# Attention scores of one head: the four products of 128 rows first, then the four of 64 rows

## The chip, the cores and the metric

The kernel runs on one NeuronCore of a Trainium2 chip. The metric is the device time of one execution in microseconds (us), as the median of several executions. Five engines work side by side, each through its own queue in order: TensorE (PE in the profile, with its weight loads as PEld), VectorE (DVE), ScalarE (ACT), GpSimd (POOL) and SyncE (SP), which here issues the DMA transfers. Products of TensorE land in PSUM, from where DVE and ACT read them.

## The reference

One layer of a decoder on 512 prompt positions and 8 single sample positions (520 columns in all), D_MODEL 1024: half a SwiGLU feed-forward block, a mixer, and half a SwiGLU block again. The mixer projects to a gated convolution (512 channels) and to attention with 8 heads of 64 channels. Three dilated patterns over the same keys are combined by their softmax masses, so for the prompt the kernel computes one masked softmax per head, in which a bias carries the logarithm of how many patterns see a key:

```
res = [dilated_band_prompt(q, k, v, w, d) for (w, d) in PATTERNS]
attn = combine_patterns([r[0] for r in res], [r[1] for r in res])
...
x = x + jnp.concatenate([y_c, y_a], axis=-1) @ w_out
```

Everything is float32, and the results have to be close to float32 accuracy.

## The kernel before, in words

Activations lie channels first: a tile has 128 channels on the partitions and positions in the columns. float32 products are made of three faster ones: each operand is split into a high part and a remainder (`hi` by ACT at L108, `lo` by DVE at L109), and `mm3` (L121 to L123) adds high·high, high·low and low·high in PSUM. Weights come through `load_w`, four raw buffers deep.

The mixer's order is written out in `ORDER`: `q`, `k`, `v`, `t` prepare a pair of heads, `C` are the three steps of a convolution block, `S` and `V` the sample's scores and values, `M` its softmax, `R` the norm of the convolution group, `O` the output projection of that group, and `A` and `B` the first and the second head of a pair. The heads come as A0, B0, A1, B1, A2, B2, A3, B3. A step with `!` is issued on TensorE only behind what was traced before it. For the rest, a scheduler that simulates a timeline sets the order on each engine, with earlier steps ahead of later ones when both are ready; the order it finds is then fixed. At the end stand `R B3 O0 O1 V1 O2 V2 V3 O3 ... O7`, then `rstd_rows` for the norm of the attention group (its chain ends in `r2`, L187) and `out_proj(4, r2)`, whose results wait for `r2` at L747.

One head (`head`) goes like this. The scores of query block `ib` (128 positions) against the keys up to its end (256, 256, 384 and 512 columns) are two products into one PSUM tile: L567 takes 128 rows, the high part of the head's 64 query channels twice over against the keys' high part and remainder; L568 takes 64 rows, the queries' remainder against the keys' high part. Blocks 0 and 1 share the tile `s01`, blocks 2 and 3 have `s2` and `s3`. The softmax of a block is a DVE pass at L575 (scale, mask, row minimum), an exponential at L577, a reciprocal and a multiplication. The transposes of L586 go to `pt` tiles, from there ACT and DVE make a high part and a remainder (L589, L590), and L594 to L597 multiply with the values into the tile `o`, which L598 and L599 read out.

All of `s01`, `s2`, `s3`, the three `pt` tiles and `o` share one tag of three PSUM buffers:

```
psS = s2.enter_context(tc.tile_pool(name="psS", bufs=3, space=PSUM, reuse_waits="tile"))
```

The tile of `R` (`one_s`, named `nps`) and that of `M` (`tp`) use the same three buffers. `R` sums a norm at L193, spreads its result back at L160, and ACT reads the tile out at L199, twice.

Of the kernel before, what the change touches and what calls it, by code (L numbers as in the profile page):

```python
# [13 lines left out]
P = 128  # L14
# [37 lines left out]
def tile_step(ctx: ExitStack, tc: tile.TileContext, xT, w0, w1a, w3a, w2a, w_in, w_out, w1b, w3b, w2b,  # L52
# [3 lines left out]
    V, A, G, PE, SP = nc.vector, nc.scalar, nc.gpsimd, nc.tensor, nc.sync  # L56
# [400 lines left out]
    with ExitStack() as st:  # L457
# [9 lines left out]
        with ExitStack() as s2:  # L467
# [90 lines left out]
            def head(e, q2, ql, k2, v2, at):  # L558
                rows = ROWS[e]
                s01 = psS.tile([P, 512], F32, name="s01", tag="s")  # L560
                s2_ = psS.tile([P, 512], F32, name="s2", tag="s")
                s3_ = psS.tile([P, 512], F32, name="s3", tag="s")
                dst = [s01[:, 0:256], s01[:, 256:512], s2_[:, 0:384], s3_[:, 0:512]]
                for ib in range(4):
                    n = max(256, P * (ib + 1))
                    i = slice(ib * P, (ib + 1) * P)
                    PE.matmul(dst[ib], lhsT=q2[e][:, i], rhs=k2[e][:, :n], start=True, stop=False)  # L567
                    PE.matmul(dst[ib], lhsT=ql[rows, i], rhs=k2[e][rows, :n], start=False, stop=True)  # L568
                mx = sm.tile([P, 4], F32, name="mx", tag="mx")
                z = sm.tile([P, 4], F32, name="z", tag="z")  # L570
                pr = []
                for ib in range(4):
                    n = P * (ib + 1)
                    p = ap.tile([P, n], F32, name=f"p{ib}", tag=f"p{ib}")
                    V.tensor_tensor_reduce(out=p, in0=dst[ib][:, :n], in1=G_[:, 384 - P * ib:512], op0=ALU.add, op1=ALU.min,  # L575
                                           scale=-0.125, scalar=-NEG, accum_out=mx[:, ib:ib + 1])
                    A.activation(p, p, AF.Exp, scale=-1.0, bias=mx[:, ib:ib + 1], accum_out=z[:, ib:ib + 1])  # L577
                    V.reciprocal(z[:, ib:ib + 1], z[:, ib:ib + 1])
                    V.tensor_scalar(p, p, z[:, ib:ib + 1], None, ALU.mult)
                    pr.append(p)  # L580
                for jb in range(4):
                    if jb < 3:
                        t = psS.tile([P, 512], F32, name="pt", tag="s")
                    o = 0 if jb < 3 else -2 * P
                    for ib in range(jb, 4):
                        PE.transpose(t[:, o + ib * P:o + (ib + 1) * P], pr[ib][:, jb * P:(jb + 1) * P], ident)  # L586
                    c = slice(jb * P - J0[jb], S - J0[jb])
                    tj = t[:, o + jb * P:o + S]
                    A.activation(pth[jb][:, c], tj, AF.Copy)  # L589
                    V.tensor_tensor(ptl[jb][:, c], tj, pth[jb][:, c].bitcast(F32), ALU.subtract)  # L590
                o = psS.tile([P, 512], F32, name="o", tag="s")
                for jb in range(4):
                    if jb:
                        PE.matmul(o[:HD, J0[jb]:], lhsT=v2[:, jb, e, :HD], rhs=ptl[jb], start=False, stop=False)  # L594
                    PE.matmul(o[:, J0[jb]:], lhsT=v2[:, jb, e], rhs=pth[jb], start=jb == 0, stop=jb == 3)
                    if not jb:
                        PE.matmul(o[:HD], lhsT=v2[:, jb, e, :HD], rhs=ptl[jb], start=False, stop=False)  # L597
                A.activation(at[rows], o[HD:], AF.Copy)  # L598
                V.tensor_tensor(at[rows], o[:HD], at[rows], ALU.add)  # L599

            def heads(hp, e):
                if not e:
                    ats[hp] = ap.tile([P, S], F32, name="at", tag="at")
                at = ats[hp]
                head(e, *qk["q", hp], qk["k", hp], vv[hp], at)
                if not e:
                    return
                add_square(at, acc_a, hp == 0, slice(0, S))
                scaled_split(at, Yh[4 + hp][:, :S], Yl[4 + hp][:, :S], GV["attn"] + hp)
# [328 lines left out]
```

## Time and profile before

| | |
|---|---|
| median of 3 executions | 1033.15 us (1032.54 to 1035.03) |
| the profiled execution's own time | 1036.0 us |
| its span, first to last instruction | 1034.2 us |
| granted TensorE clock, mean | 0.981 |
| PE busy | 996.0 us, 96% of the span |
| DVE busy | 726.5 us, 70% |
| ACT busy | 505.0 us, 49% |
| POOL busy | 92.2 us, 9% |

The mixer's heads lie between about 420 and 607 us of the span. Products are pipelined on TensorE: the duration of one in a timeline is longer than the distance from its start to the start of the next, and it is this distance that tells how long TensorE was taken. In a row of a timeline the first number is the start, the second the duration, and `64*128 64x256` means weights of 64 rows by 128 columns and 256 moving columns.

### The profile page before, as it was taken

The numbers are of one execution on the slowest core, as the hardware profiler recorded it, in microseconds if no ns is written. First come the engines' busy times: TensorE is split into PE (matmuls) and PEld (weight loads), VectorE is DVE, ScalarE is ACT, GpSimd is POOL, SyncE is SP. The second block draws the span as 40 slices with busy tenths as digits, with TensorE's granted clock in tenths as the row PEclk, the third lists the DMA queues.
The fourth block names the chain that finished last, engine by engine and source line by source line (L and its number), as shares of the span: only waits on it lengthen the run. The fifth ranks groups of instructions, "written<-read, shape, count | busy, mean of one in ns | idle before, by whom it ended". The sixth has DMA issues, their size and how long they took to land.

```text
span 1034.2 us, 19174 instructions
## 1 busy us (share of the span) xinstructions
PE 996.0 (96%) x7897; PEld 965.4 (93%) x7897; DVE 726.5 (70%) x1193; ACT 505.0 (49%) x833; POOL 92.2 (9%) x103
## 2 busy tenths in 40 slices
PE   6999999999999999999999998999999999999997
PEld 5999999999999999999999897999998999999897
DVE  6788888436786546667688799797887634788332
ACT  4534565323555436566565545443555422555342
POOL 1000000000000031112022263000000000000022
PEclk6999999999999999999999999999999999999998
DMA  6325434354443445243246665325334233333302
GB/s 208 113 90 186 144 131 140 105 183 156 148 157 125 143 141 173 83 144 129 66 146 222 205 203 184 103 82 184 133 125 151 64 90 113 102 103 103 101 22 83
DMA packets 37912, 136.62 MB, mean 132 GB/s; under 512 B 5760, under 2 KB 8512, under 8 KB 37312
## 3 DMA queue, kind: packets, MB, share of 16 engines
q1 hardware_dynamic: 37824, 135.39, 39.2%
q8 instruction: 62, 1.02, 0.4%
q14 instruction: 26, 0.21, 0.1%
HBM read 131.07 MB, written 37.82 MB: 163 GB/s over the span
## 4 chain that ended last, share of the span: by engine, by line
PE 70%; DVE 15%; DMA 6%; issue 4%; ACT 4%; POOL 1%; SPq 0%; POOLq 0%; DVEq 0%; ACTq 0%
PE ps L121 22%; PE ps L123 21%; PE ps L122 21%; DVE lo L373 3%; DMA raw<-in_w1b 2%; DVE lo L109 2%; DMA raw<-in_w3b 2%; DVE ls L373 1%; ACT hi L108 1%; PE s L568 1%; DMA raw<-in_w1a 1%; DVE ws L364 1%; DVE raw L365 1%; ACT hi L372 1%; DVE ws L363 1%
## 5 line engine op out<-in xcount | busy, mean ns | idle before, releaser
L108 ACT ACTIVATE hi<-raw 128x1024 fp32r<-128x1024 f32 (+3 forms) x136 | 119.1, 878 | 215.6 <-PE ps L122 167.3
L121 PE MATMUL ps<-hh,hi 128*128 128x260 f32 x704 | 200.5, 287 | 4.3 <-ACT hi L108 3.5
L123 PE MATMUL ps<-hh,lo 128*128 128x260 f32 x704 | 200.8, 286 | 1.5 <-DVE lo L109 1.4
L122 PE MATMUL ps<-hl,hi 128*128 128x260 f32 x704 | 199.9, 285 | 0.5 <-DVE hl L300 0.3
L109 DVE TENSOR_TENSOR lo<-raw,hi 128x1024 fp32r<-128x1024 f32 (+3 forms) x136 | 143.6, 1057 | 74.9 <-ACT hi L108 74.0
L121 PEld LDWEIGHTS ps<-hh,hi 128*128 128x128 f32 x704 | 133.5, 191 | 6.8 <-ACT hi L108 4.3
L123 PEld LDWEIGHTS ps<-hh,lo 128*128 128x128 f32 x704 | 134.0, 190 | 3.0 <-DVE lo L109 2.5
L122 PEld LDWEIGHTS ps<-hl,hi 128*128 128x128 f32 x704 | 134.0, 190 | 1.2 <-DVE hl L300 1.2
L121 PE MATMUL ps<-mh,hi 128*128 128x260 f32 x384 | 110.3, 288 | 1.8 <-DVE q L498 1.1
L123 PE MATMUL ps<-mh,lo 128*128 128x260 f32 x384 | 109.3, 285 | 0.3 <-DVE u L619 0.3
L122 PE MATMUL ps<-ml,hi 128*128 128x260 f32 x384 | 109.4, 285 | 0.0
L372 ACT ACTIVATE hi<-raw 128x1024 fp32r<-128x1024 f32 x72 | 75.7, 1053 | 60.8 <-PE ps L122 58.2
L144 POOL TENSOR_TENSOR acc<-acc,sq 128x520 f32<-128x520 f32 (+1 forms) x25 | 38.3, 1530 | 752.9 <-ACT sq L143 748.8
L373 DVE TENSOR_TENSOR lo<-raw,hi 128x1024 fp32r<-128x1024 f32 x72 | 87.5, 1217 | 4.8 <-ACT hi L372 4.8
L372 ACT ACTIVATE hs<-ws 128x1024 fp32r<-128x1024 f32 x72 | 60.5, 840 | 54.0 <-DVE ws L364 48.0
L121 PE MATMUL ps<-f1sh,hi 128*128 128x260 f32 x288 | 82.1, 285 | 3.4 <-DVE X L404 1.2
L121 PE MATMUL ps<-f0sh,hi 128*128 128x260 f32 x288 | 82.2, 286 | 2.0 <-ACT a L384 1.7
L122 PE MATMUL ps<-f0sl,hi 128*128 128x260 f32 x288 | 81.4, 283 | 0.0
L123 PE MATMUL ps<-f1sh,lo 128*128 128x260 f32 x288 | 80.2, 282 | 1.3 <-DVE lo L373 1.2
L122 PE MATMUL ps<-f1sl,hi 128*128 128x260 f32 x288 | 81.3, 283 | 0.0
L123 PE MATMUL ps<-f0sh,lo 128*128 128x260 f32 x288 | 79.6, 282 | 0.0
L404 DVE SCALAR_TENSOR_TENSOR X<-ps,X 128x260 f32<-128x260 f32 x96 | 36.7, 422 | 57.9 <-PE ps L123 57.9
(278 smaller groups left out, 2744.8 us busy)
## 6 DMA issues: line engine op xcount, KB each, us to landing
out_cko<-in_ck SPq DMA_DIRECT2D x16, 1023.0 KB, 7.1
out_cvo<-in_cv SPq DMA_DIRECT2D x16, 1023.0 KB, 7.2
raw<-in_w_in SPq DMA_DIRECT2D x24, 512.0 KB, 3.3
raw<-in_w1b SPq DMA_DIRECT2D x22, 512.0 KB, 3.3
raw<-in_w3b SPq DMA_DIRECT2D x22, 512.0 KB, 3.3
raw<-in_w3a SPq DMA_DIRECT2D x21, 512.0 KB, 3.3
raw<-in_w1a SPq DMA_DIRECT2D x20, 512.0 KB, 3.3
raw<-in_w2a SPq DMA_DIRECT2D x16, 320.0 KB, 3.0
```

The costliest lines, as they stand in the source:

```text
L108: A.activation(hi, raw, AF.Copy)
L109: V.tensor_tensor(lo, raw, hi.bitcast(F32), ALU.subtract)
L121: PE.matmul(out, lhsT=hi, rhs=xh, start=start, stop=False, skip_group_check=more)
L122: PE.matmul(out, lhsT=hi, rhs=xl, start=False, stop=False, skip_group_check=more)
L123: PE.matmul(out, lhsT=lo, rhs=xh, start=False, stop=stop, skip_group_check=more)
L144: G.tensor_tensor(dst[:, c], dst[:, c], sq[:, c], ALU.add)
L363: V.tensor_tensor(s[:, 0], rb[:, :KQ], rb[:, KQ:], ALU.add)
L364: V.tensor_tensor(s[:, 1], s[:, 0], ra[:, :KQ], ALU.add)
L365: V.tensor_tensor(rb[:, :KQ], rb[:, :KQ], ra[:, :KQ], ALU.add)
L372: A.activation(h, f, AF.Copy)
L373: V.tensor_tensor(l, f, h.bitcast(F32), ALU.subtract)
L404: V.scalar_tensor_tensor(X[m][:, c], ps[:, h, :TH], 0.5, X[m][:, c], ALU.mult, ALU.add)
```

## The change

The eight products of a head keep their operands and their destinations. The loop now runs twice over the four blocks: first the four products of 128 rows, then the four of 64 rows. Each of the last seven is tied by `keep_in_program_order` to TensorE's product traced just before it, so it can't be issued ahead of that one; other instructions may still come in between. Since `s01` holds two blocks, block 1's first product no longer starts with a clearing of the tile (`start=ib != 1`): the flag of block 0 covers the tile, and two checks of the language on open groups are switched off.

```
-                for ib in range(4):
-                    n = max(256, P * (ib + 1))
-                    i = slice(ib * P, (ib + 1) * P)
-                    PE.matmul(dst[ib], lhsT=q2[e][:, i], rhs=k2[e][:, :n], start=True, stop=False)
-                    PE.matmul(dst[ib], lhsT=ql[rows, i], rhs=k2[e][rows, :n], start=False, stop=True)
+
+                for low in range(2):
+                    for ib in range(4):
+                        n = max(256, P * (ib + 1))
+                        i = slice(ib * P, (ib + 1) * P)
+                        if low:
+                            mm = PE.matmul(dst[ib], lhsT=ql[rows, i], rhs=k2[e][rows, :n], start=False, stop=True,
+                                           skip_group_check=ib < 2)
+                        else:
+                            mm = PE.matmul(dst[ib], lhsT=q2[e][:, i], rhs=k2[e][:, :n], start=ib != 1, stop=ib < 2,
+                                           skip_group_check=ib == 1)
+                        if low or ib:
+                            tc.keep_in_program_order(mm)
```

## Rows read from the trace of the kernel before

**Rows 1.** The page: busy time of TensorE, and its granted clock in 40 slices of the span.

```profile
PE 996.0 (96%) x7897; PEld 965.4 (93%) x7897; DVE 726.5 (70%) x1193; ACT 505.0 (49%) x833; POOL 92.2 (9%) x103
PEclk6999999999999999999999999999999999999998
```

**Rows 2.** TensorE's waits, from 420 to 582 us (the first two rows) and from 582 to 645 us (two of the four there). Columns: us in total, times, the longest.

```profile
PE ps L123 <- DVE u L619: 0.3, 1, 0.3
PE nps L193 <- POOL acc L144: 0.2, 1, 0.2
...
PE ps L121 <- ACT f1h L135: 2.9, 1, 2.9
...
PE ps L121 <- DVE t L747: 0.2, 1, 0.2
```

**Rows 3.** The timeline of TensorE over the scores of head A0, and the two products behind them.

```profile
420.79 0.28 PE L567 MATMUL s<-k,q 128*128 128x256 f32 x1
421.00 0.38 PE L568 MATMUL s<-k,ql 64*128 64x256 f32 x1
421.31 0.38 PE L567 MATMUL s<-k,q 128*128 128x256 f32 x1
421.63 0.38 PE L568 MATMUL s<-k,ql 64*128 64x256 f32 x1
421.94 0.44 PE L567 MATMUL s<-k,q 128*128 128x384 f32 x1
422.31 0.44 PE L568 MATMUL s<-k,ql 64*128 64x384 f32 x1
422.68 0.50 PE L567 MATMUL s<-k,q 128*128 128x512 f32 x1
423.11 0.50 PE L568 MATMUL s<-k,ql 64*128 64x512 f32 x1
423.54 0.39 PE L121 MATMUL ps<-mh,hi 128*128 128x260 f32 x1
423.77 0.28 PE L122 MATMUL ps<-ml,hi 128*128 128x260 f32 x1
```

**Rows 4.** The same timeline, products of the head's output, all of 128 rows (the second and the third with 64 weight columns).

```profile
435.96 0.39 PE L595 MATMUL o<-pth,v 128*128 128x512 f32 x1
436.19 0.39 PE L597 MATMUL o<-ptl,v 128*64 128x512 f32 x1
...
436.65 0.34 PE L594 MATMUL o<-ptl,v 128*64 128x384 f32 x1
436.83 0.34 PE L595 MATMUL o<-pth,v 128*128 128x384 f32 x1
```

**Rows 5.** The instructions of lines 567 and 568: count, duration in ns (least, median, most), first and last start, forms with their counts.

```profile
L567 PE MATMUL s<-k,q x32: 279/385/502, 420.8 to 587.0; 128*128 128x256 f32 x16, 128*128 128x384 f32 x8, 128*128 128x512 f32 x8
L568 PE MATMUL s<-k,ql x32: 377/410/501, 421.0 to 587.3; 64*128 64x256 f32 x16, 64*128 64x384 f32 x8, 64*128 64x512 f32 x8
```

**Rows 6.** The timeline from 603 to 608 us: four transposes of 64 rows, one behind the other, with their weight loads (merged into one row each).

```profile
605.84 0.32 PEld L728 LDWEIGHTS ot<-ident,os__6958 64*128 64x128 f32 x4
605.84 0.46 PE L728 MATMUL ot<-ident,os__6958 64*128 64x64 f32 x4
```

**Rows 7.** Head B0: the timeline of TensorE (the last products of A0's output, and B0's product of 512 columns), then that of DVE.

```profile
443.35 0.28 PE L594 MATMUL o<-ptl,v 128*64 128x256 f32 x1
443.47 0.28 PE L595 MATMUL o<-pth,v 128*128 128x256 f32 x1
...
447.61 0.40 PE L567 MATMUL s<-k,q 128*128 128x512 f32 x1
...
444.10 0.29 DVE L575 CUSTOM_DVE_ANT_0 p<-s,G__4336 128x128 f32<-128x128 f32 x1 [0.27 <-PE s L568]
...
444.83 0.56 DVE L575 CUSTOM_DVE_ANT_0 p<-s,G__4336 128x384 f32<-128x384 f32 x1
...
445.43 0.69 DVE L545 TENSOR_TENSOR ql<-q,q 64x512 fp32r<-64x512 f32 x1
...
449.69 0.67 DVE L599 TENSOR_TENSOR at<-o,at 64x512 f32<-64x512 f32 x1
```

**Rows 8.** The end of head A3 and the last head, B3, in the timelines of the engines: DVE's readout of A3's output, `R` and the products of B3 on TensorE, DVE's pass over B3's block 3, ACT's two readouts of `R`'s tile, and ACT's first instruction of the norm of the attention group.

```profile
573.42 0.68 DVE L599 TENSOR_TENSOR at<-o,at 64x512 f32<-64x512 f32 x1
...
581.26 1.08 PE L193 MATMUL nps<-ones,acc 128*104 128x1 f32 x10 [0.20 <-POOL acc L144]
582.20 0.36 PE L567 MATMUL s<-k,q 128*128 128x256 f32 x1
...
587.01 0.40 PE L567 MATMUL s<-k,q 128*128 128x512 f32 x1
...
588.26 0.68 DVE L575 CUSTOM_DVE_ANT_0 p<-s,G__4336 128x512 f32<-128x512 f32 x1
...
593.14 0.39 ACT L199 ACTIVATE acc<-nps 128x260 f32<-128x260 f32 x1 [0.79 <-PE nps L160]
...
607.47 1.91 POOL L144 TENSOR_TENSOR acc_a<-acc_a,sq 128x512 f32<-128x512 f32 x2 [0.31 <-ACT sq L143]
...
612.46 0.64 ACT L171 ACTIVATE rhi<-acc_a 128x520 fp32r<-128x520 f32 x1 [0.40 <-POOL acc_a L144]
```

## The prediction

> **What bounds the kernel now.** I read the page first. TensorE is busy for 96% of the span, and at the full of its two clock levels (2.4 GHz) in all slices but the first and the last [rows 1]. Then its waits: from 420 to 582 us, where seven of the eight heads lie, it waits for other engines 0.5 us in all [rows 2]. So this stretch ends when TensorE's queue ends, and time taken out of the queue is time gained there, as long as other work is ready to move up. Behind it one wait matters. The attention group's norm reaches L747 when TensorE has just run out of other work, and it waits 0.2 us; the 2.9 us wait further on belongs to the next block and moves with whatever comes before it [rows 2]. So in the mixer's end two things finish together, TensorE's work and the chain of the last head, and a gain has to move both.
>
> Next I read the timeline of head A0, for the distance from start to start [rows 3]. From the first score product to the second product behind the last, 2.98 us pass. What would the same nine products take undisturbed? Products of 512 and 384 columns that follow one another without a change of form stand 0.23 and 0.18 us apart [rows 4], those of 256 columns 0.12 [rows 7], and those of 260 the same. That makes 2 x (0.12 + 0.12 + 0.18 + 0.23) + 0.12 = 1.42 us. So 1.56 us are extra, and they appear each time the weights' rows change between 128 and 64, on the way in and on the way out: eight changes, 0.195 us each. That it is the change, and not adding into the same PSUM tile, is seen from L594 and L595, which add into one tile 0.12 us apart [rows 7], and from the projection's product behind the last score, which shares no tile with it and is still followed at 0.23 instead of 0.12 [rows 3].
>
> **The change part by part.**
>
> *Changes of form.* There are 32 products of 64 rows [rows 5], each alone between products of 128 rows: 64 changes. Afterwards a head has one way in and one way out: 16. It saves 48 x 0.195 = 9.4 us, 1.17 per head, 8.2 by the time A3 is done. The products, their columns and their PSUM writes stay as they are.
>
> *Within the run of 64 rows.* No two score products of 64 rows follow each other now. The nearest rows are four transposes of 64 rows: together 0.46 us with the last one's end, their four weight loads 0.32 us [rows 6], so a following one starts within 0.1 us, though each loads 128 columns of weights. I take the undisturbed distances also here; the bounds are no extra, and the exposed load that a product behind a change shows, 0.23 - 0.12 = 0.11 us [rows 3], three times per head. A rule of the Trainium skill speaks for the second: "TensorE: Matmul & The Clock Gate", Part 3, says that a weight load overlaps products in flight only when it goes to another row group, and all four go to the same. By it 24 loads of 0.11 us would stay exposed, and 6.8 us would be saved instead of 9.4. The transposes share one row group too, and four loads in 0.32 us beside four products in 0.46 leave little exposed: the trace is against the rule.
>
> *The order ties.* They cost no instruction. They forbid that block 3's first product waits while blocks 0 to 2 go ahead, and that matters for the buffers. Seven tiles of a head turn through three buffers. In B0, block 3's product starts at 447.61, blocks 0 to 2 having been read out from 444.10 to 445.43, while A0's output tile is read until 449.69 + 0.67 = 450.36 [rows 7]. With three buffers, block 3 must have got the buffer of `s01` or `s2`, not that of A0's output. After the change these two are complete only behind block 3's first product, so it has to wait for the third buffer: for the previous head's output to be read out. TensorE doesn't stand still, since earlier or later steps' products move up; but all four softmaxes of the head start behind that point. Within a head this is bounded by 0 (the readout at L598 and L599 comes early enough) and by 450.36 - 447.61 = 2.8 us plus the 1.3 us of the three DVE passes that used to run ahead (444.10 to 445.43) plus 0.5 us for the three products in front: 4.6 us. Up to A3 I take no loss, because B3 starts 582.20 - 574.10 = 8.1 us after A3's output is read [rows 8], set by `R` and with it by TensorE's progress, and the chain may use that up.
>
> *The last head.* For B3 the third buffer is that of `R` (`nps`): L193 takes it at 581.26 and L199 reads it last until 593.53, while B3's block 3 went ahead at 587.01 [rows 8]. Now it has to stay behind. `R` moves up by the 8.2 us to 573.1; 12.3 us later, at 585.3, the buffer is free. Then 0.23 for block 3's first product, 0.2 for the change, 0.12 to block 1's second product and 0.28 for its end: 586.1; three passes on DVE (1.3) and block 3's pass starts at 587.5. It stood at 588.26 [rows 8], so the chain gains only 0.8 us. Behind it lies some slack: POOL's sums are done at 607.47 + 1.91 = 609.4, and ACT takes them up at 612.46 [rows 8]; of these 3.1 us I count 2.1, since the sample's part and POOL's other updates fill the rest. The norm would come 2.9 us earlier, TensorE's work 9.4: it would stand still for 6.5. That is the upper bound of what is given back, the lower is 0. Between the two, `R`'s 12.3 us hold work of B3 that leaves this stretch: its pairs took 1.9 and 0.86 us of TensorE (distances of [rows 3]), and 0.4 stays. With 2.3 us off, 4.2 are given back. I take this, as it comes from rows of this very place.
>
> *Sum.* 9.4 - 4.2 = 5.2 us. The profiled execution took 1036.0 us, 1.8 more than its span; it becomes 1030.8. The median shown is 2.85 us below that execution, so I set the saving against the median: 1033.15 - 5.2 = 1028.0.
>
> **The rivals.**
>
> 1. *All is kept.* If `R` is through quickly, or B3's third buffer comes from elsewhere, nothing is given back: 1033.15 - 9.4 = 1023.8. For it: nearly all waits of TensorE in this stretch are zero. Against it: three buffers for two norms and a head.
> 2. *The chain of heads becomes the bound, and the kernel slower.* A1 to A3 follow one another closely, and each waits for the buffer of the one before. If the five of them lose 2.8 us each, as the readout of A0's output stood in B0, A3 ends 14.0 us later, and B3 starts 14.0 - 8.1 = 5.9 us later than now, with TensorE out of work: 1039. It decides from 8.1 us on, 1.6 per head. For it: the rows of B0. Against it: the late readout there was ACT's order, which a scheduler that needs the buffer may change.
> 3. *The middle of this.* The heads lose 1 to 1.6 us each: the chain is then where it was, and the time within 3 us of 1033.
> 4. *The change doesn't do what it says.* The ties hold the eight in order, not together. If the scheduler puts another product of 128 rows between the four of 64 in most heads, half the changes stay: 4.7 saved, less 4.2, 1032.6. Against it: the four have nothing to wait for once block 3's first product is out.
> 5. *The loads stay exposed*, by the rule above: 24 x 0.11 = 2.6 us less, 1028.0 + 2.6 = 1030.6.
>
> **How the numbers follow.** A measurement can't tell less than 0.3% (3.1 us) from no change, so faster means below 1030.05. The forecast, with 3.1 to 8 us saved (1025.2 to 1030.0), gets 0.42; rival 1 gets 0.22, rival 2 0.14, rival 3 0.08, rival 4 0.09, rival 5 0.05. Faster are the forecast and rival 1: 0.64. Rivals 3, 4 and 5 are no change: 0.22. Rival 2 is slower: 0.14. The range runs from 1022.5 (all kept, and 1.3 us below it for the scatter of a median, half of what the three executions span) to 1035.5, which leaves out rival 2 and a little below; the forecast's own range is 1025.2 to 1030.0.
>
> **What would show it.** In the changed kernel's timeline a head's run of four 64-row products should have starts about 0.12, 0.12 and 0.18 us apart (0.11 more each by rival 5), and a distance of about 0.3 us only on the way in and out. L567 should show 24 of 32 durations near 0.28 to 0.40. In B0, the 512-column product should start behind A0's L599; in B3, behind the second L199. In the waits of TensorE, L747 should rise from 0.2 to about 4 us: near 0 means rival 1, and a wait ahead of B3 means rival 2. The prediction is wrong if the distances inside the run of 64 rows are as large as before, or if the time falls by less than 3 or by more than 8 us.

## The result, and the profile after

The changed kernel is slower: 1045.77 us median (1041.67 to 1046.85, 6 executions) against 1033.75 (1031.87 to 1040.89) for the kernel before, which was run again beside it. The ratio is 1.0101, with a 95% interval of 1.0068 to 1.0135. Forecast were 1028.0 us, and the range ended at 1035.5. Its profiled execution took 1046.33 us, with a span of 1044.5; that is 10.3 more than the span before. In the lines of the changed file, L573 and L570 are the products of 128 and of 64 rows (L567, L568 before), L583 is the softmax pass (L575), L594 a transpose of scores (L586), L602 to L605 are the output products (L594 to L597), L607 is the output's readout (L599) and L755 the wait for the norm (L747).

The page, busy time of TensorE and the granted clock in 40 slices [rows 1]:

```profile
PE 994.1 (95%) x7897; PEld 966.9 (93%) x7897; DVE 720.5 (69%) x1193; ACT 504.9 (48%) x833; POOL 92.5 (9%) x103
PEclk6999999999999999999997998999999999999998
```

The busy sum fell by only 1.9 us, although 9.4 us of work went: two slices now stand at a lower clock, where the same products take longer (sums below). The waits of TensorE, from 420 to 582 us (six rows) and from 582 to 660 (three) [rows 2]:

```profile
PE s L573 <- DVE at L607: 2.6, 1, 2.6
PE pt L594 <- DVE p L587: 2.2, 1, 2.2
PE ps L123 <- DVE lo L109: 1.1, 2, 0.7
PE pt L594 <- DVE u L627: 0.8, 1, 0.8
PE pt L594 <- DVE ss L690: 0.5, 1, 0.5
PE sc L684 <- DVE skq L659: 0.3, 1, 0.3
...
PE ps L121 <- DVE t L755: 5.1, 1, 5.1
PE ps L121 <- ACT f1h L135: 2.1, 1, 2.1
...
PE s L573 <- ACT acc L199: 0.3, 1, 0.3
...
```

Among the heads TensorE waited 0.5 us before. Now it waits 8.0 (with two rows of 0.3 and 0.2 not shown), and first of all for the readout of an output: `s L573 <- DVE at L607` is block 3's first product waiting for the previous head's tile. Three rows of transposes (`pt L594`, 3.5 in all) wait for DVE, which is then at the head's softmaxes and at work of other steps. The wait at the norm has grown from 0.2 to 5.1 us.

The scores of head A0 [rows 3], the four of a kind merged into one row:

```profile
420.67 0.81 PE L573 MATMUL s<-k,q 128*128 128x256 f32 x4
421.40 0.91 PE L570 MATMUL s<-k,ql 64*128 64x256 f32 x4
422.24 0.39 PE L121 MATMUL ps<-mh,hi 128*128 128x260 f32 x1
422.47 0.28 PE L122 MATMUL ps<-ml,hi 128*128 128x260 f32 x1
```

From 420.67 to 422.47 are 1.80 us, where 2.98 stood. So the change does what it says. Its cost is seen in the timelines of all engines, at B0, at A3 and at B3 [rows 7, 8], and at the norm:

```profile
447.93 0.68 DVE L607 TENSOR_TENSOR at<-o,at 64x512 f32<-64x512 f32 x1
...
450.40 0.39 PE L573 MATMUL s<-k,q 128*128 128x512 f32 x1
...
451.25 0.29 DVE L583 CUSTOM_DVE_ANT_0 p<-s,G__4336 128x128 f32<-128x128 f32 x1
...
452.90 0.68 DVE L583 CUSTOM_DVE_ANT_0 p<-s,G__4336 128x512 f32<-128x512 f32 x1
...
559.29 0.34 PE L573 MATMUL s<-k,q 128*128 128x384 f32 x1
...
560.28 1.23 DVE L109 TENSOR_TENSOR lo<-raw,hi 128x1024 fp32r<-128x1024 f32 x1 [2.44 <-ACT hi L108]
...
561.53 0.68 DVE L607 TENSOR_TENSOR at<-o,at 64x512 f32<-64x512 f32 x1
...
562.27 0.80 PE L573 MATMUL s<-k,q 128*128 128x512 f32 x1 [2.64 <-DVE at L607]
...
563.83 0.29 DVE L583 CUSTOM_DVE_ANT_0 p<-s,G__4336 128x128 f32<-128x128 f32 x1 [1.61 <-PE s L570]
...
566.77 0.88 PE L594 MATMUL pt<-ident,p 128*128 128x128 f32 x3 [2.23 <-DVE p L587]
...
581.79 0.67 DVE L607 TENSOR_TENSOR at<-o,at 64x512 f32<-64x512 f32 x1
...
585.30 0.99 PE L193 MATMUL nps<-ones,acc 128*104 128x1 f32 x10
...
594.63 0.37 ACT L199 ACTIVATE acc<-nps 128x260 f32<-128x260 f32 x1
595.05 0.49 PE L573 MATMUL s<-k,q 128*128 128x512 f32 x1 [0.30 <-ACT acc L199]
...
597.74 0.68 DVE L583 CUSTOM_DVE_ANT_0 p<-s,G__4336 128x512 f32<-128x512 f32 x1
...
633.02 0.70 DVE L755 TENSOR_TENSOR t<-ps,r 128x520 f32<-128x520 f32 x1
...
634.65 0.42 PE L121 MATMUL ps<-Yh,hi 128*128 128x260 f32 x1
634.87 0.42 PE L122 MATMUL ps<-Yl,hi 128*128 128x260 f32 x1
```

At A3 one sees the whole chain. The 384-column product of 128 rows is out at 559.29. Block 3's has to wait for B2's output, read until 562.21, and starts at 562.27. The first of the four softmax passes comes at 563.83, the first transpose at 566.77, and TensorE has nothing else in between. A3's output is read at 582.46, and was at 574.10 before [rows 8]: 8.4 us later, although the heads up to it have saved 8.2 us of TensorE's work. In the last head block 3's product stands 0.05 us behind the second readout of `R`'s tile.

The same in all heads (us; starts of block 3's first product, and the end of the previous head's readout, from the same timelines):

| head | before: readout, block 3 | after: readout, block 3 |
|---|---|---|
| B0 | 450.4, 447.6 | 448.6, 450.4 |
| A1 | 466.0, 469.7 | 469.3, 471.6 |
| B1 | 492.7, 495.1 | 492.5, 494.8 |
| A2 | 513.0, 511.9 | 516.2, 518.0 |
| B2 | 536.8, 534.3 | 538.7, 541.1 |
| A3 | 555.4, 552.1 | 562.2, 562.3 |

Before, block 3 went ahead of that readout in four heads of six; now it is behind it in every one, by up to 2.4 us. Only in A3 does TensorE stand still for it. In the other five heads it is busy in between, in B0 for all 1.90 us from 448.60 to 450.50: the order found beforehand has other products there.

TensorE by stretches of 4 us (columns: stretch and its length, then busy time and count of PE, PEld, DVE, ACT, POOL, the granted clock, DMA share, GB/s):

```profile
560.00:564.00 4.00, 1.73 (x5) 1.21 (x5) 2.08 (x3) 2.58 (x5) 1.04 (x1) 0.76 0.35 121
564.00:568.00 4.00, 1.48 (x6) 0.55 (x5) 4.00 (x18) 2.93 (x10) 1.48 (x2) 0.50 0.03 10
568.00:572.00 4.00, 2.66 (x12) 2.06 (x13) 4.00 (x11) 1.91 (x4) 2.27 (x2) 0.50 0.01 2
572.00:576.00 4.00, 4.00 (x21) 4.00 (x21) 3.90 (x9) 1.60 (x4) 0.35 (x1) 0.53 0.02 1
576.00:580.00 4.00, 4.00 (x32) 3.73 (x32) 1.13 (x5) 0.88 (x3) 0.00 (x0) 1.00 0.00 0
...
628.00:632.00 4.00, 0.53 (x3) 0.30 (x2) 2.71 (x6) 1.55 (x3) 0.00 (x0) 0.79 0.41 128
632.00:636.00 4.00, 2.13 (x10) 2.17 (x11) 3.75 (x6) 0.64 (x1) 0.00 (x0) 0.50 0.16 61
636.00:640.00 4.00, 4.00 (x31) 4.00 (x31) 1.50 (x3) 1.27 (x2) 1.30 (x1) 0.85 0.01 2
```

After the waits the clock stands at its lower level (1.2 GHz), for some 12 us among the heads and again behind the norm, where two products of 260 columns follow each other in 0.22 us (634.65, 634.87) instead of 0.12. That is a second price of such a wait. DVE, on the other hand, is busy without a pause from 564 to 572 us: the four softmaxes of A3 now come together.

**Where the time went.** `R` starts at 585.30, and by the forms alone it would have moved from 581.26 [rows 8] to 573.1: 12.2 us to be explained. Of them, 7.5 are more waiting (8.0 - 0.5), and some 4.4 the lower clock (an estimate: busy time times what is missing from 1.00, in the four stretches from 560 to 576: 0.4 + 0.7 + 1.3 + 1.9). Behind `R` the span grows by a further 10.3 - 4.0 = 6.3: the wait at L755 by 4.9, the lower clock from 628 to 640 by 1.8 in the same way, and 1.2 less for the six changes that B3 saves. That makes 5.5; 0.8 I can't place.

### The profile page after: what moved, and what is told of

Read it like the earlier page. It is cut to its first block, busy times and chain, and to the rows that moved or that the text cites. A ratio compares the mean times of both kernels' runs of the same rounds, so it can differ in the third digit from the quotient of the medians.

```text
span 1044.5 us, 19179 instructions
## 1 busy us (share of the span) xinstructions
PE 994.1 (95%) x7897; PEld 966.9 (93%) x7897; DVE 720.5 (69%) x1193; ACT 504.9 (48%) x833; POOL 92.5 (9%) x103
## 4 chain that ended last, share of the span: by engine, by line
PE 73%; DVE 13%; ACT 5%; DMA 4%; issue 4%; SPq 1%; POOL 0%; POOLq 0%; DVEq 0%; ACTq 0%
PE ps L121 23%; PE ps L123 23%; PE ps L122 23%; DVE lo L373 2%; DVE lo L109 2%; ACT hi L108 1%; DMA raw<-in_w1b 1%; DVE ls L373 1%; DMA raw<-in_w1a 1%; ACT hi L372 1%; PE pt L594 1%; DVE ws L364 1%; DMA raw<-in_w3b 1%; DVE raw L365 1%; DMA raw<-in_w3a 1%
## 5 line engine op out<-in xcount | busy, mean ns | idle before, releaser
L108 ACT ACTIVATE hi<-raw 128x1024 fp32r<-128x1024 f32 (+3 forms) x136 | 118.8, 877 | 216.0 <-PE ps L122 170.1
L109 DVE TENSOR_TENSOR lo<-raw,hi 128x1024 fp32r<-128x1024 f32 (+3 forms) x136 | 140.1, 1033 | 80.1 <-ACT hi L108 79.8
L121 PEld LDWEIGHTS ps<-mh,hi 128*128 128x128 f32 x384 | 73.4, 191 | 4.1 <-issue 1.9
```

The costliest lines, as they stand in the source:

```text
L108: A.activation(hi, raw, AF.Copy)
L109: V.tensor_tensor(lo, raw, hi.bitcast(F32), ALU.subtract)
L121: PE.matmul(out, lhsT=hi, rhs=xh, start=start, stop=False, skip_group_check=more)
```

## The experiments

Theory: what costs the time is that block 3 must stay behind the tile it needs, with all four softmaxes of the head behind it. Rivals: the products themselves are dearer in the new order; the last head alone is to blame; or the tied order costs something that has nothing to do with the buffer. The first of these falls with A0's 1.80 us above. Ratios are to the kernel before, from executions on the same chip, with their 95% interval. The number of form changes comes from the order of TensorE's instructions.

**1. The new loops without the ties.** Only block 1's first product stays tied, which it must be, since block 0's flag clears its tile. 40 changes of form remain.

```
-                        if low or ib:
+                        if not low and ib == 1:
```

> The new loop order, but only block 1's first product is tied behind block 0's. The scheduler may then let the products of 64 rows of blocks 0 to 2 go before block 3's first product. In its fixed order the form changes 40 times, against 64 before and 16 in the changed kernel. Theory B (buffers: block 3's first product has to wait for the third buffer of the tag, held by the head before or by R, and four softmaxes wait behind it): the wait goes, 24 changes of 0.195 us are saved, so 1033.75 - 4.7 = 1029.1, ratio 0.9955, and TensorE no longer stands idle between 555 and 580 us nor at the norm of the attention group (5.1 us). Theory G (the grouping itself costs: products of 64 rows in a run, or the softmaxes that start close together): still slower than before, above 1037.

1028.67 us, 0.9949 (0.9933 to 0.9966), 5.3 us less. Its waits of TensorE, same two stretches:

```profile
PE ps L123 <- DVE u L627: 0.3, 1, 0.3
PE nps L193 <- POOL acc L144: 0.2, 1, 0.2
...
PE ps L121 <- ACT f1h L135: 2.9, 1, 2.9
```

The waits among the heads and the one at the norm are gone, and 24 changes x 0.195 = 4.7 us come off in full. Of all kernels tried this is the fastest, ahead of both that were compared.

**2. The wait alone.** The pairs of before, all 64 changes; but two products of one column into `s2` and `s3`, overwritten later, stand tied between block 0's two.

```
+                    if not ib:
+                        for t in (s2_, s3_):
+                            tc.keep_in_program_order(PE.matmul(t[:, :1], lhsT=ones, rhs=ones[:, 0:1], start=True, stop=True))
-                    PE.matmul(dst[ib], lhsT=ql[rows, i], rhs=k2[e][rows, :n], start=False, stop=True)
+                    mm = PE.matmul(dst[ib], lhsT=ql[rows, i], rhs=k2[e][rows, :n], start=False, stop=True)
+                    if not ib:
+                        tc.keep_in_program_order(mm)
```

> The order of pairs of the kernel before, 64 changes of form, and only the wait added: behind block 0's first product two products of one column (they write a column that is overwritten later) claim the tiles of blocks 2 and 3, and block 0's second product is tied behind them. So all three buffers must be free before any softmax of the head can start, as in the changed kernel, and nothing is grouped. Theory B: the cost of the wait without the gain: the changed kernel lost 12.0 us net, and 9.4 us of changes saved are in that, so about 21 us, 1050 to 1058, ratio 1.016 to 1.024, with TensorE idle behind A2 and A3 and at the norm of the attention group. Theory G: within 0.3% of the kernel before.

1043.31 us, 1.0092 (1.0068 to 1.0116): 9.5 us more, without any change of form saved. So taking the buffers early is enough to make the kernel nearly as slow as the changed one, though two things keep this from being the wait alone. The added products take time: in A0 block 0's second product stands 0.55 us behind its first, where it stood 0.21 [rows 3], which makes some 2.7 us in eight heads (an estimate). And in the seven heads from B0 on, block 2's pair comes ahead of the second added product, so that three softmaxes stand behind it and not four; in B0 that product starts at 445.37, before A0's output is read (448.53). I had expected more, the changed kernel's loss plus its saving, and a wait at the norm, which isn't there. The two don't add: among the heads TensorE waits 3.0 us here and 8.0 in the changed kernel, as it would if time taken out of its queue turned into waiting where the chain of heads is the bound. Its stretches, columns as above:

```profile
564.00:568.00 4.00, 3.12 (x18) 2.29 (x18) 4.00 (x13) 1.93 (x7) 0.65 (x1) 1.00 0.22 85
568.00:572.00 4.00, 1.79 (x12) 1.19 (x12) 3.86 (x11) 2.66 (x5) 2.34 (x2) 0.84 0.01 2
572.00:576.00 4.00, 4.00 (x18) 4.00 (x19) 4.00 (x9) 1.67 (x4) 0.45 (x1) 0.50 0.40 132
```

The hole and the fall of the clock stand at the same place, in the heads' last pair.

**3. Orders between the two.** The eight as `(low, ib)`, tied one behind the other; in the first one only blocks 0 and 1 are tied.

```
+                for low, ib in ((0, 0), (0, 1), (1, 0), (1, 1), (0, 2), (1, 2), (0, 3), (1, 3)):
```

> Only blocks 0 and 1, which share a tile, are grouped (128, 128, 64, 64), and blocks 2 and 3 stay pairs; 50 changes of form in the fixed order instead of 64. Theory B: no product waits for a buffer that it didn't wait for before, so 14 x 0.195 = 2.7 us are saved: 1031.0, ratio 0.9973 (0.995 to 0.999). Theory G: the softmaxes start as before and only two products of 64 rows follow each other, so 1033 to 1036.

1030.18 us, 0.9975 (0.9956 to 0.9994), as expected: 50 changes, 2.6 us less.

```
+                for low, ib in ((0, 0), (0, 1), (1, 0), (1, 1), (0, 2), (0, 3), (1, 2), (1, 3)):
```

> Order blocks 0 and 1 of 128 rows, blocks 0 and 1 of 64 rows, then blocks 2 and 3 of 128 rows, blocks 2 and 3 of 64 rows, all tied. 34 changes instead of 64: 30 x 0.195 = 5.9 us. Blocks 0 and 1 are complete before block 3's product, so their softmaxes run ahead of the wait for the third buffer; block 2's is behind it. The run with three and one, where two of the three tiles were also complete only behind the third's wait or just ahead of it, ended at 1.0032 instead of 0.994; the run with one pair and singles at 0.9975. My theory (what counts is how many softmaxes stand behind the wait for the third buffer): between these, ratio 0.998 to 1.004. Rival (only the number of changes counts, plus one wait in the last head): 0.9943 to 0.998.

1031.18 us, 0.9992 (0.9970 to 1.0015): within what my theory gave and above the rival's range, though its interval reaches into that range; so this run alone doesn't exclude the rival.

```
+                for low, ib in ((0, 0), (0, 1), (0, 2), (1, 0), (1, 1), (1, 2), (0, 3), (1, 3)):
```

> Blocks 0, 1, 2 with 128 rows, then blocks 0, 1, 2 with 64 rows, all tied, and then block 3's pair; 32 changes of form instead of 64. Theory B: block 3 can take the buffer of blocks 0 and 1 again, so 32 x 0.195 = 6.2 us are saved, less some where block 2's first product waits for its own buffer (in A2 and A3 it stood 3 to 4 us behind block 1's in the kernel before): 1027.5 to 1031, ratio 0.994 to 0.997. Theory G: slower than before, about half way to the changed kernel or more (1038 to 1045).

1035.66 us, 1.0032 (1.0011 to 1.0053), a miss. I had thought of block 3's buffer alone; but here blocks 0 and 1 are complete only behind block 2's first product, and that one stands 3 to 5 us behind block 1's in A2, B2 and A3. Side by side (saved: changes less than 64, times 0.195; the last column is the time from A0's first product to the end of A3's readout in the timeline, 153.3 in the kernel before):

| order | changes | behind another block's first product | saved, us | measured, us | A0 to A3, us |
|---|---|---|---|---|---|
| no ties | 40 | none | 4.7 | -5.3 | 149.3 |
| a pair, then singles | 50 | none | 2.7 | -2.6 | 151.0 |
| two and two | 34 | block 2 | 5.9 | -0.8 | 153.3 |
| three, then one | 32 | blocks 0 and 1 | 6.2 | +3.3 | 155.1 |
| the change, four and four | 16 | blocks 0 to 2 | 9.4 | +10.4 | 161.8 |

The more softmaxes stand behind another block's first product, the more is lost, and with two or more of them more than the forms give. The last column shows that this happens among the heads. In the first two orders A3 comes earlier by just the changes that are gone up to there (20 x 0.195 = 3.9 and 12 x 0.195 = 2.3 us, measured 4.0 and 2.3). In the others 26, 28 and 42 changes are gone, and A3 comes 0.0, 1.8 and 8.5 us later.

**4. `R`'s tile from elsewhere.** The last head then needn't wait for `R`.

```
-            one_s = lambda: [psS.tile([P, 512], F32, name="nps", tag="s")] * 2
+            one_s = lambda: [psM.tile([P, 2, 512], F32, name="nps", tag="mm")[:, 0]] * 2
```

> The changed kernel with the tile of R taken from the projections' pool instead of the three buffers, so in B3 block 3's first product waits only for A3's output and no longer for R's second readout (it stood at 595.05 in the changed kernel, behind blocks 0 to 2 at 586.2). Theory B: block 3 of B3 at about 587, the chain of the last head 8 us earlier, the wait at the norm of the attention group (5.1 us, and the half clock behind it) gone: 1037 to 1041, less what R costs in the projections' two buffers. Theory G: no change, 1043 to 1049.

1041.08 us, 1.0072 (1.0045 to 1.0098), at the upper edge of what was expected; the traced execution took 1036.46, the shortest of the six. All engines' timeline at B3:

```profile
579.11 0.67 DVE L607 TENSOR_TENSOR at<-o,at 64x512 f32<-64x512 f32 x1
...
579.84 0.76 PE L573 MATMUL s<-k,q 128*128 128x384 f32 x2 [1.13 <-DVE at L607]
...
583.32 0.90 PE L193 MATMUL nps<-ones,acc 128*104 128x1 f32 x9
```

B3 no longer stands behind `R`, and the wait at the norm is gone; but it stands behind A3's readout, as every head does. The time falls by 3.0 us by the ratios, whose intervals overlap; most of the loss stays. Up to A3 the timeline is as it was: 161.9 us from A0's first product to the end of A3's readout, against 161.8 in the changed kernel and 153.3 before. So the last head alone isn't to blame. The same edit without the ties:

> The kernel without the ties (loops as in the change, one tie for block 1's first product), and R's tile from the projections' buffers as in the run that moved it alone. 46 changes instead of 40, so 64 - 46 = 18 changes x 0.195 = 3.5 us less than before: ratio 0.9966 if R's place matters only where the ties force block 3 to wait. If the last head still waited for R's buffer without the ties, up to 4 us more come off: 0.993.

1035.68 us, 1.0030 (1.0009 to 1.0052), a miss: 8.4 us more than without the edit (its trace has 42 changes, not 46). Both kernels with the moved tile wait 2.0 and 1.2 us for splits of weights behind 582 us, rows that the kernel without ties doesn't have. Taking a buffer from the projections has a price of its own, so experiment 4 gives no clean size for the last head.

**5. A fourth buffer**, by merging the sample's own PSUM buffer (tag `x`) into the heads' three; in the changed kernel, in the one before, and in that without ties.

```
-            psS = s2.enter_context(tc.tile_pool(name="psS", bufs=3, space=PSUM, reuse_waits="tile"))
+            psS = s2.enter_context(tc.tile_pool(name="psS", bufs=4, space=PSUM, reuse_waits="tile"))
...
-                vt = psS.tile([P, 4, 2, HD], F32, name="vt", tag="x", bufs=1)
+                vt = psS.tile([P, 4, 2, HD], F32, name="vt", tag="s")
```

> The changed kernel with a fourth buffer under the tag of the score tiles: the bank of the tag x joins it, and the tiles that used it (vt, and the sample's sc and so, which stay for long) take turns with the rest. 16 changes of form as in the changed kernel. Theory B: up to A2, where the sample's scores begin to hold the fourth buffer, block 3's first product no longer waits for the output of the head before, so the heads from B0 to A2 come 2 to 6 us earlier than in the changed kernel; behind that the wait is back. Faster than the changed kernel by 5 to 14 us: 1031 to 1040, against 1045.8. Theory G: the grouping is unchanged, so within 0.3% of the changed kernel, 1043 to 1049.

> The control: the kernel before with the same fourth buffer, 64 changes of form. TensorE hardly waits from 420 to 645 us in the kernel before, so a fourth buffer should give nothing by either theory: 1030 to 1036, within 0.3%.

> Both: the fourth buffer, and the ties taken away but for block 1's first product. 30 changes of form instead of 64, 10 fewer than with three buffers. Theory B: 34 x 0.195 = 6.6 us less than before and no wait added: 1026.6, ratio 0.9936 (0.991 to 0.997). Theory G: not faster than the version without ties and with three buffers (0.9949).

1047.0 us, 1.0131 (1.0101 to 1.0161); 1042.62, 1.0094 (1.0065 to 1.0122); 1037.67, 1.0039 (1.0016 to 1.0062): all three missed, since the control shows that sharing the sample's buffer costs 9.7 us by itself. Against that control the tied order is 3.8 us slower by the ratios, whose intervals overlap, though it has 48 changes fewer. In its timeline block 3 follows block 0 in 0.4 to 0.7 us in B0, A1 and B1 (440.20 and 440.84 in B0) and later again in A2, B2 and A3 (5.4, 5.6 and 1.7 us). But in all six heads it stands ahead of the previous head's last readout. So that wait is gone up to A3, and still the tied order gains nothing there: 139.9 us from A0's first product to A3's readout, 140.1 in the control, though 42 changes fewer would make 8.2. TensorE's transposes wait for the softmaxes instead (`pt L594 <- DVE p L587`, 5.7 us in four times; 1.4 in two times in the control). That fits the rival that the tied order costs something by itself.

**6. The output's tile apart.** The tile `o` takes the sample's buffer, in the changed kernel and in the one before, so that block 3 needn't wait for the previous head's readout.

```
-                o = psS.tile([P, 512], F32, name="o", tag="s")
+                o = psS.tile([P, 512], F32, name="o", tag="x", bufs=1)
```

> The changed kernel with one edit: the output tile `o` of a head comes from the tag of the sample's tiles (`x`, one buffer) and not from the three buffers of the scores. Block 3's first product then never waits for the previous head's readout; only for its third `pt` tile, which is free some 3 us earlier. 32 changes of form instead of 16, because other products now come between. The output's tile has to wait for the sample's tiles, which may cost something of its own; the control beside it has the same edit in the old order. My theory (the wait for the previous head's readout is what the changed kernel loses by up to A3): this kernel is 2 to 6 us faster than the control (32 changes less are 6.2 us, less up to 4 us of the wait for R's tile in the last head), and block 3's product stands ahead of the previous head's last readout in most heads. Rival (it is the tied order as such, with all softmaxes behind all eight products): it stays 5 us or more slower than the control.

> Control: the kernel before with the same edit, the output tile from the sample's buffer. 64 changes of form as before. If the sample's buffer is free when a head's output wants it, ratio 0.995 to 1.002; each wait for it shows as time above that, and the kernel with the new order has it too.

1050.13 us, 1.0168 (1.0140 to 1.0196), and the control 1048.21, 1.0145 (1.0115 to 1.0176). The times don't tell the two apart, and the sample's buffer costs some 15 us in the old order: a miss. The timelines tell more, for the heads up to A3. The changed order first (A3's block 3, B2's readout, A3's readout, then B3), then the control (A3's readout, then B3):

```profile
537.10 0.40 PE L573 MATMUL s<-k,q 128*128 128x512 f32 x1
...
539.12 0.68 DVE L607 TENSOR_TENSOR at<-o,at 64x512 f32<-64x512 f32 x1
...
551.86 0.68 DVE L607 TENSOR_TENSOR at<-o,at 64x512 f32<-64x512 f32 x1 [1.41 <-ACT at L606]
...
602.13 0.39 ACT L199 ACTIVATE acc<-nps 128x260 f32<-128x260 f32 x1 [1.00 <-PE nps L160]
...
603.56 0.40 PE L573 MATMUL s<-k,q 128*128 128x512 f32 x1
...
605.72 0.28 DVE L583 CUSTOM_DVE_ANT_0 p<-s,G__4336 128x128 f32<-128x128 f32 x1
```

```profile
552.66 0.68 DVE L599 TENSOR_TENSOR at<-o,at 64x512 f32<-64x512 f32 x1 [1.63 <-ACT at L598]
...
597.02 0.28 DVE L575 CUSTOM_DVE_ANT_0 p<-s,G__4336 128x128 f32<-128x128 f32 x1
...
603.91 0.69 DVE L575 CUSTOM_DVE_ANT_0 p<-s,G__4336 128x512 f32<-128x512 f32 x1 [1.71 <-PE s L568]
```

With the output's tile out of the way, block 3 stands ahead of the previous readout again (537.10 and 539.12; so in all six heads from B0 to A3), and A3's output is read 0.8 us earlier than in the control (551.86, 552.66), where with the shared tile it was 8.4 us later than before. So the long delay goes with the tile. But the tied order isn't free of cost: its trace has 16 changes, not the 32 that I expected, and 42 fewer than the control up to A3, which would make 8.2 us; counted from A0's first product, A3's output comes only 1.8 us earlier (132.1 and 133.9). From 420 to 582 us TensorE waits 12.2 us, in the control 7.3, and the longest row is one that the control doesn't have:

```profile
PE pt L594 <- DVE p L587: 3.7, 4, 1.6
```

The transposes wait for four softmaxes that start together. What is left is the last head: B3's first softmax pass stands behind block 3, which stands behind `R`'s tile, and comes at 605.72 instead of 597.02, so that B3's output is read 4.5 us later than in the control (625.5 and 621.0). The wait at the norm is 4.7 us here and 0.4 in the control, much as it was 5.1 in the changed kernel and 0.2 before; with the fourth buffer it is 4.7, and its control has no such row.

## Why the prediction was wrong, point by point

- *Changes of form, 0.195 us each, 1.17 per head*: right. A0's nine products take 1.80 us, 2 changes above the undisturbed 1.42 make 1.81; and the kernel without ties has its 4.7 us, the one with a pair its 2.7.
- *Loads in the run of 64 rows*: right, not exposed. From the first of them to the projection's product behind, 0.84 us pass (421.40 to 422.24), which the undisturbed distances and one change give (0.12 + 0.12 + 0.18 + 0.23 + 0.195 = 0.85); three exposed loads would make it 1.17. Rival 5 falls, and with it, for this case, the rule as it stands in the Trainium skill, "TensorE: Matmul & The Clock Gate", Part 3, that a load overlaps products in flight only when it goes to another row group: all four go to the same one. Rival 4 falls too: 16 changes are left.
- *The ties*: the mechanism was right. Block 3 stands behind the previous head's readout, and the four softmaxes stand behind block 3. That four softmaxes starting together cost something even without that wait was not in it.
- *"Up to A3 I take no loss, because B3 starts 582.20 - 574.10 = 8.1 us after A3's output is read"*: this is the step that failed. A3's output comes 8.4 us later than before, where TensorE's work was to be 8.2 us ahead: 16.6 us apart, twice what the 8.1 could cover. Those 8.1 us were TensorE's other work between the readout and B3; once TensorE is 8.2 us ahead, they are used up before the chain has lost anything. I counted the slack for the chain of heads and the saving for TensorE, and they are the same time.
- *TensorE doesn't stand still, since other products move up*: right up to 558 us, where the waits add up to 1.2 us (0.7, 0.3 and 0.2, the same view for that stretch), and wrong behind it, where the other 6.8 lie. The other work was moved up into the heads' waits, and in the last pair there was none left.
- *The last head*: the mechanism and its place were right. `R`'s tile was held 585.30 to 595.00, 9.7 us, where 12.3 - 2.3 = 10.0 were taken; block 3 stands right behind L199; and L755 waits 5.1 us where about 4 were forecast.
- *Rival 2* is what happened, priced at 1039 with a chance of 0.14. Its condition (1.6 us lost per head) was met, though unevenly: from B0 to A3 block 3 stands 2.8, 1.9, -0.3, 6.1, 6.8 and 10.1 us later than before. It had A3 end 14.0 us later, where 8.4 were measured, and B3 start 5.9 us later, where 4.0 were (586.16 - 582.20). The lower clock ahead of `R`, some 4.4 us, was in no rival. What rival 2 lacked besides are the 6.3 us behind: the last head's wait, which I had only in the forecast, and the clock once more. What I set against it, that ACT's order could change, didn't help: at A3, B2's last output product starts at 559.17, but ACT and DVE split weights first (DVE's L109, 560.28 to 561.51, behind ACT's L108), and the readout ends at 562.21.

## What to carry to other kernels

A tie in the order of an in-order engine is also a tie in the order of its buffers: list for each tied instruction which tile it must get, who reads that tile last, and what of the same group is then held behind it. Where an engine is 96% busy, the slack of the chain beside it is measured in the time that one means to save; take the saving off the slack first, and see who is the bound then. Tie only what correctness needs, and let the rest find its place: here, of the orders with the buffers left as they were, the one with the fewest form changes was the slowest and the one with 40 of 64 the fastest.

## What the runs showed of the hardware

I hadn't counted on the clock. A head's wait is not over when TensorE goes on: from 564 to 576 us, behind 4 us of which TensorE was busy for 1.73, the granted clock was 0.50 to 0.53, and 4.00 us of busy time held 21 products where 576 to 580 at 1.00 held 32. In the kernel with the wait alone it fell to 0.50 at the same place. And the cost of a change of form is the same 0.195 us, whichever order surrounds it: in A0 eight changes gave 1.56 us before, and two gave 0.38 after (1.80 - 1.42).

Three things stay open. How the 10.4 us split between the middle heads and the last one isn't settled, since both ways of moving a tile cost time of their own (8.4 us with the projections' buffer, some 10 to 15 with the sample's). How much of the heads' loss is the wait for the previous readout, and how much the four softmaxes that start together, was not tried apart: without that wait the tied order gained 0.2 and 1.8 us of 8.2 up to A3, with it A3 came 8.5 later. And why the sample's buffer is so dear was not tried.
